# A hybrid diffusion backbone: transposes of the modulation chunks in a rotating PSUM bank

## The chip, the cores and the metric

The kernel runs on one core of one Trainium2 chip. The metric is the device time of one execution in microseconds (us); the number of a kernel is the median of its runs. The engines are called by the names of the profile: PE (matmul), PEld (its weight load), DVE, ACT, POOL, and the queues that issue DMAs (SPq, ACTq).

## The reference

One inference step through two layers of a diffusion backbone with a model width of 2048. There are 256 tokens: 128 of context and 128 latent ones. Cut to what matters here:

```
for l in range(2):
    mods = SiLU([c_ctx, c]) @ ada_w[l] + ada_b[l]      # 2 x 12288: shift, scale, gate, twice
    u    = rmsnorm(x) * (1 + scale1) + shift1
    p    = u @ w_in[l]                                 # columns of three head groups
    y    = [attention(p), gated_delta_rule(p), ssd_scan(p)]
    x    = x + gate1 * (concat(y) @ w_out[l])
    x    = x + gate2 * swiglu_ffn(rmsnorm(x) * (1 + scale2) + shift2)
```

The modulation is a product of two rows (one for context tokens, one for latent tokens) with a 2048 x 12288 matrix per layer, 96 MB of weights in each layer. The other weights (`w_in`, `w_out`, the feed-forward matrices) are streamed from HBM too, and each is used once.

## The kernel before, in words

**Weights.** A weight tile (`raw`, 512 KB) is loaded through SPq into a ring of four. ACT copies it into a rounded tile (L360), DVE or POOL takes the residual (L364), and PE multiplies the tokens with both into one of four PSUM banks `acc`. These matmuls, `acc<-h,w` in the profile, fill most of PE's time.

**Modulation.** Its columns are cut into 48 chunks of 256 columns for each layer. The first 16 of layer 0 are done ahead of the layer, most of the others as sums on DVE. The 24 chunks 16 to 39 of layer 0 are done on PE in the mixers of layer 0, between other work. One chunk is 16 matmuls `ada<-araw,sc`: four weight tiles `araw` of 512 KB with four matmuls each (`ada_run`). The four row groups of the result land in the first half of one PSUM bank, `pz["sums"]`, whose tile is named `ada`. Then ACT copies the sums to one buffer `adsb` in SBUF (L422), and the chunk is pending. `ada_flush` finishes a pending chunk: two PE transposes of `adsb` (L435) into a PSUM tile `pm`, a DVE reduction into `mods` (L436), a DVE sum with the bias (L437).

**When chunks run.** `tick` is called in the loops of the mixers: it flushes the pending chunk and then runs more of the next one by a credit. The matmul stream of the program, DVE's and the other engines' are then ordered by a scheduler, which places each instruction from what it needs and what is free; so a changed dependency can change the order of an engine. What this order is can be listed without running the kernel.

**The `araw` tiles.** There are eight of them: two in the pool of the weights and six in a pool `am`, which is released at the end of the delta rule. The tiles of the attention part (`cr`, `sqa`, `sqb`) then take its place, so the DVE copies of attention's first projection (L1178) wait until the last of the six has been read. From there on two tiles are left.

**PSUM.** Eight banks: four of `acc`, one of the sums, three that rotate, allocated by `mx()`. All the small products of the mixers (state-space scan, delta rule, attention) use the three, each tile until its reader has finished.

**The mixers in order of time (layer 0).** The state-space scan (`u,xd` and `bt,xd` products, from 204 us); inputs of the delta rule: norms by `t,ones`, ACT L613, decay factors `E` (DMA L874, DVE L879), then `Bp` (DVE L1039); its 16 x 16 inverse, done by DVE alone (L1047 to L1058), with transfers to DRAM and back on both sides (`sB`, `Lr` ahead, `sZ`, `sW`, `Z`, `W` behind); the solve, a chain of `Z,Bp`, `t,W` and `W,t` products (L1094 to L1111) with chunks between; outputs (`E,Z`, `qe,s`, `t,ones`); then attention (`sqa,ones`, `usT,cst`, `krd,cst`).

Of the kernel before, what the change touches and what calls it, by code (L numbers as in the profile page):

```python
# [182 lines left out]
def build(tc, nc, a):  # L183
# [5 lines left out]
    def nm(s):  # L189
        uid[0] += 1  # L190
        return f"{s}_{uid[0]}"
# [6 lines left out]
    pz = {}  # L198
# [16 lines left out]
    def mx():  # L215
        return pz["mx"].tile([128, 512], F32, name=nm("mx"), tag="mx")
# [60 lines left out]
    def C(name):  # L277

        if name == "ident":
            return ident  # L280
        o, w = _COFF[name]
        return cst["t"][:, o:o + w]
# [5 lines left out]
    def cr(l, name, n):  # L288
        o = _COLS[name]
        return cols[:, l, o:o + n]  # L290
# [107 lines left out]
    def ada_run(n):  # L398


        i = ada_state["i"]
        if i >= ada_state["stop"]:
            return
        l, c = ada_q[i]
        if ada_state["u"] == 0:
            ada_state["ps"] = pz["sums"][:, 0:256]
        ps = ada_state["ps"]
        ada_fetch(n - len(ada_state["raws"]))

        for u in range(ada_state["u"], ada_state["u"] + n):  # L410
            raw = ada_state["raws"].pop(0)
            for j in range(4):
                mm(ps[32 * j:32 * j + 32], sc[:, 4 * u + j, :], raw[:, j, :], u == 0, u == 3)
                pinned["on"] = True
        pinned["on"] = False
        ada_state["u"] += n
        if ada_state["u"] == 4:
            ada_flush()
            ada_state["u"] = 0
            ada_state["i"] += 1  # L420
            sb = wp.tile([128, 256], F32, name=nm("adsb"), tag="adsb", bufs=1)
            S.activation(sb, ps, AF.Copy)  # L422
            ada_state["pend"] = l, c, sb

    def ada_flush():

        if ada_state["pend"] is None:
            return
        l, c, sb = ada_state["pend"]
        ada_state["pend"] = None  # L430
        pm = pz["sums"][:, 256:512]
        md = mods[l][:, 2 * c:2 * c + 2, :]
        bias = cr(l, "adab", 96)[:, 2 * c:2 * c + 2].unsqueeze(2).to_broadcast([128, 2, 2])
        for t in range(2):
            PE.transpose(pm[:, t * 128:(t + 1) * 128], sb[:, t * 128:(t + 1) * 128], C("ident"))  # L435
        V.tensor_reduce(md, pm.rearrange("p (t j r) -> p t r j", t=2, j=4)[:, :, 0:2, :], axis=AX.X, op=ALU.add)  # L436
        V.tensor_tensor(md, md, bias, op=ALU.add)  # L437
        scale_rows(l, 2 * c, 2 * c + 2)

    def scale_rows(l, a0, a1):  # L440

        for w, o in enumerate((16, 64)):
            b0, b1 = max(a0, o), min(a1, o + 16)
            if b0 < b1:
                gain = cr(l, "n1" if w == 0 else "n2", 16)[:, b0 - o:b1 - o].unsqueeze(2).to_broadcast([128, b1 - b0, 2])
                V.scalar_tensor_tensor(modA[l][w][:, b0 - o:b1 - o, :], mods[l][:, b0:b1, :], 1.0, gain, op0=ALU.add, op1=ALU.mult)
# [84 lines left out]
    def tick(n=1.0):  # L531
        credit[0] += rate[0] * n
        if "s" in pz:
            while credit[0] >= 1.0:
                credit[0] -= 1.0
                vec_step()
            return
        ada_flush()
        while credit[0] >= ada_state["run"]:
            credit[0] -= ada_state["run"]  # L540
            ada_run(ada_state["run"])
# [33 lines left out]
    def ada_until(l, c):  # L575

        while ada_state["i"] < ada_state["stop"] and ada_q[ada_state["i"]] < (l, c):
            ada_run(2)
        if ada_state["pend"] is not None and ada_state["pend"][:2] < (l, c):
            ada_flush()  # L580
# [1007 lines left out]
```

## Time and profile before

| | |
|---|---|
| median of three runs | 2791.19 us (2787.31 to 2797.09) |
| profiled execution | 2789.01 us, span 2787.2 us, 1.8 us around the span |
| PE busy | 2624.7 us, 94% of the span |
| DVE, ACT, POOL busy | 1924.1, 1261.9, 753.6 us |
| matmuls of the chunks, `ada<-araw,sc` | 88.3 us on PE, with 21.1 us of idle time before them |
| mixers of layer 0, where the chunks run | 204 to about 670 us of the span |

How to read it: PE's share is so high that the time is PE's work and PE's waits. The idle time before the chunk matmuls is the time in which PE had arrived at such a matmul and could not start it. The profile counts each 32-bit matmul in two records, so that one chunk is 32 records of `ada<-araw,sc`.

### The profile page before, as it was taken

The numbers are of one execution on the slowest core, as the hardware profiler recorded it, in microseconds if no ns is written. First come the engines' busy times: TensorE is split into PE (matmuls) and PEld (weight loads), VectorE is DVE, ScalarE is ACT, GpSimd is POOL, SyncE is SP. The second block draws the span as 40 slices with busy tenths as digits, with TensorE's granted clock in tenths as the row PEclk, the third lists the DMA queues.
The fourth block names the chain that finished last, engine by engine and source line by source line (L and its number), as shares of the span: only waits on it lengthen the run. The fifth ranks groups of instructions, "written<-read, shape, count | busy, mean of one in ns | idle before, by whom it ended". The sixth has DMA issues, their size and how long they took to land. (4 is left out here: it accounts for less than half of the span.)

```text
span 2787.2 us, 45955 instructions
## 1 busy us (share of the span) xinstructions
PE 2624.7 (94%) x17856; PEld 2324.3 (83%) x17856; DVE 1924.1 (69%) x3162; ACT 1261.9 (45%) x1802; POOL 753.6 (27%) x415
## 2 busy tenths in 40 slices
PE   7988889999999999999999999999999999999999
PEld 5876767888887788788888888888988888888888
DVE  2657845454999899898986786555477777755444
ACT  4345605544444444444334563355454454444333
POOL 1121003222455555455554320231330000000000
PEclk9999999999999999999999999999999999999999
DMA  8988757456698888889985555343657777655554
GB/s 331 347 305 289 251 185 243 151 212 222 230 323 313 312 299 318 294 307 337 340 322 186 172 163 169 111 137 110 221 194 230 232 241 229 202 187 188 195 195 149
DMA packets 224107, 658.01 MB, mean 236 GB/s; under 512 B 34320, under 2 KB 61584, under 8 KB 223888
## 3 DMA queue, kind: packets, MB, share of 16 engines
q1 hardware_dynamic: 174384, 619.26, 64.1%
q10 hardware_dynamic: 49504, 35.81, 4.3%
q8 instruction: 140, 2.29, 0.3%
q14 instruction: 79, 0.65, 0.1%
HBM read 641.22 MB, written 13.76 MB: 235 GB/s over the span
## 5 line engine op out<-in xcount | busy, mean ns | idle before, releaser
L225 PE MATMUL acc<-h,w 128*128 128x256 f32 (+1 forms) x8960 | 1428.9, 320 | 54.2 <-DVE w L364 19.0
L225 PEld LDWEIGHTS acc<-h,w 128*128 128x128 f32 x8960 | 1273.2, 193 | 205.6 <-DVE w L364 29.0
L360 ACT ACTIVATE w<-raw 128x1024 fp32r<-128x1024 f32 (+2 forms) x811 | 828.6, 1025 | 889.1 <-PE acc L225 606.5
L364 DVE TENSOR_TENSOR w<-raw,w 128x1024 fp32r<-128x1024 f32 (+2 forms) x577 | 710.5, 1232 | 512.5 <-ACT w L360 503.6
L364 POOL TENSOR_TENSOR w<-raw,w 128x1024 fp32r<-128x1024 f32 (+3 forms) x234 | 569.2, 2434 | 993.1 <-ACT w L360 840.2
L505 DVE SCALAR_TENSOR_TENSOR junk<-araw,srep 128x1024 bf16<-128x1024 f32 x448 | 544.5, 1215 | 9.6 <-DMA araw<-ada_w 1.9
L225 PE MATMUL acc<-f,w 128*128 128x256 f32 (+1 forms) x2560 | 456.3, 340 | 3.6 <-DVE w L364 3.6
L225 PEld LDWEIGHTS acc<-f,w 128*128 128x128 f32 x2560 | 392.8, 189 | 64.3 <-DVE w L364 4.3
L225 PE MATMUL acc<-m,w 128*128 128x256 f32 x1536 | 191.8, 285 | 0.0
L225 PEld LDWEIGHTS acc<-m,w 128*128 128x128 f32 x1536 | 186.6, 192 | 2.9 <-issue 2.5
L1424 POOL TENSOR_TENSOR f<-sg,f 128x512 fp32r<-128x512 f32 x40 | 60.9, 1523 | 426.3 <-ACT f L1423 426.3
L225 PE MATMUL ada<-araw,sc 128*32 128x256 f32 x1280 | 88.3, 397 | 21.1 <-DVE mods L436 16.2
L225 PE MATMUL mx<-h,w 128*128 128x256 f32 (+1 forms) x672 | 90.7, 293 | 10.1 <-ACT w L360 5.2
L225 PEld LDWEIGHTS mx<-h,w 128*128 128x128 f32 (+1 forms) x672 | 85.7, 195 | 14.6 <-ACT w L360 6.2
L661 DVE SCALAR_TENSOR_TENSOR xT<-acc,mods,xT 128x128 f32<-128x128 f32 x192 | 53.9, 343 | 43.1 <-PE acc L225 35.5
L225 PEld LDWEIGHTS ada<-araw,sc 128*32 128x32 f32 x1280 | 37.6, 112 | 51.8 <-DVE mods L436 18.1
L1428 ACT ACTIVATE up<-acc 128x256 f32<-128x256 f32 x80 | 30.7, 384 | 107.6 <-PE acc L225 76.4
L648 ACT ACTIVATE h<-nt,mods 128x128 fp32r<-128x128 f32 x128 | 44.0, 392 | 63.7 <-DVE nt L647 62.5
L647 DVE SCALAR_TENSOR_TENSOR nt<-xT,modA,rstd 128x128 f32<-128x128 f32 x128 | 57.0, 482 | 7.4 <-ACT rstd L611 7.2
L1428 ACT ACTIVATE sg<-acc 128x256 f32<-128x256 f32 x80 | 29.9, 381 | 68.4 <-PE acc L225 68.4
L602 POOL TENSOR_TENSOR sqacc<-sqacc,sqt 128x256 f32<-128x256 f32 x39 | 39.9, 1022 | 74.0 <-ACT sqt L598 73.1
L1463 DVE TENSOR_TENSOR sg<-sg,up 128x256 f32<-128x256 f32 x80 | 57.8, 723 | 1.6
(296 smaller groups left out, 1971.6 us busy)
## 6 DMA issues: line engine op xcount, KB each, us to landing
araw<-ada_w SPq DMA_DIRECT2D x384, 512.0 KB, 5.4
raw<-ffn_w_gu SPq DMA_DIRECT2D x352, 512.0 KB, 4.4
raw<-ffn_w_down SPq DMA_DIRECT2D x165, 512.0 KB, 4.3
raw<-w_in SPq DMA_DIRECT2D x144, 512.0 KB, 4.6
raw<-w_out SPq DMA_DIRECT2D x64, 512.0 KB, 4.0
raw<-mla_w_uq SPq DMA_DIRECT2D x24, 384.0 KB, 3.1
raw<-mla_w_ukv SPq DMA_DIRECT2D x16, 512.0 KB, 3.7
araw<-srow SPq DMA_DIRECT2D x12, 512.0 KB, 5.7
```

Source lines behind the costliest of these rows:

```text
L225: return pin(PE.matmul(out, lhsT=lhsT, rhs=rhs, start=start, stop=stop, skip_group_check=True))
L360: S.activation(w1[:, :w], raw[:, :w], AF.Copy)
L364: e.tensor_tensor(w2[:, :w], raw[:, :w], f32(w1[:, :w]), op=ALU.subtract)
L505: V.scalar_tensor_tensor(junk, raw, 1.0, s[r], op0=ALU.mult, op1=ALU.mult, accum_out=sums[g][:, 2 * (c - g[1]) + t, r, h:h + 1]))
L602: G.tensor_tensor(sq["acc"], sq["acc"], t, op=ALU.add)
L647: V.scalar_tensor_tensor(t[:, c], X_["t"][:, kt, c], A[:, kt, g:g + 1], rstd[:, c], op0=ALU.mult, op1=ALU.mult)
L648: S.activation(h1[:, kt, c], t[:, c], AF.Identity, bias=B[:, kt, g:g + 1])
L661: V.scalar_tensor_tensor(xs, ps[:, i * T:(i + 1) * T], gates[:, kt, g:g + 1], xs, op0=ALU.mult, op1=ALU.add)
L1424: G.tensor_tensor(f[:, :, 1], sg_, f32(f[:, :, 0]), op=ALU.subtract)
L1428: S.activation(t, bank[:, NT:2 * NT], AF.Copy)
L1463: V.tensor_tensor(t[:, j], t[:, j], u, op=ALU.mult)
```

## The change

The PSUM tile that takes the two transposes of a finished chunk is no longer the second half of the bank of the running sums; it is a fresh tile of the three rotating banks. Nothing else in the text of the program differs:

```
 def ada_flush():
     ...
     l, c, sb = ada_state["pend"]
     ada_state["pend"] = None
-    pm = pz["sums"][:, 256:512]
+    pm = mx()[:, 0:256]
     md = mods[l][:, 2 * c:2 * c + 2, :]
     ...
     for t in range(2):
         PE.transpose(pm[:, t * 128:(t + 1) * 128], sb[:, t * 128:(t + 1) * 128], C("ident"))
     V.tensor_reduce(md, pm.rearrange(...), axis=AX.X, op=ALU.add)
```

The counts of instructions are the same, but for two table loads fewer on ACT. The order of the engines changes in the mixers of layer 0; from their end on it is the same. Three places follow; a suffix such as `x4` is the number of matmuls, and numbers behind names count tiles.

The first is PE around the wait for the inverse: the last inputs `qT,kT`, and the first product of the solve, `Z,Bp`. Before:

```order
L435 MATMUL ada_70<-ident,adsb_3216 128x128 x2
L225 MATMUL ada_70<-araw_3274,sc 32x256 x4
L225 MATMUL ada_70<-araw_3276,sc 32x256 x4
L225 MATMUL ada_70<-araw_3278,sc 32x256 x4
L225 MATMUL ada_70<-araw_3280,sc 32x256 x4
L435 MATMUL ada_70<-ident,adsb_3298 128x128 x2
L225 MATMUL ada_70<-araw_3455,sc 32x256 x4
L225 MATMUL ada_70<-araw_3457,sc 32x256 x4
L225 MATMUL ada_70<-araw_3459,sc 32x256 x4
L225 MATMUL ada_70<-araw_3461,sc 32x256 x4
L225 MATMUL mx_3006<-Z_2936,Bp_2839 128x128 x4
L225 MATMUL mx_3013<-t_3011,W_2937 128x128 x4
```

And now:

```order
L225 MATMUL mx_2999<-qT_244,kT_245 128x128 x4
L225 MATMUL mx_3006<-qT_244,kT_245 128x128 x4
L225 MATMUL acc_4087<-h_236,w_667_4332 128x256 x2
L225 MATMUL acc_4087<-h_236,w_668_4333 128x256
L225 MATMUL mx_3013<-Z_2943,Bp_2846 128x128 x4
L225 MATMUL mx_3020<-t_3018,W_2944 128x128 x4
L225 MATMUL mx_3026<-W_2944,t_3018 128x128 x4
L435 MATMUL mx_3032<-ident,adsb_2708 128x128 x2
L225 MATMUL mx_3037<-Z_2947,Bp_2859 128x128 x4
L225 MATMUL ada_70<-araw_3201,sc 32x256 x4
L225 MATMUL ada_70<-araw_3203,sc 32x256
```

Three chunks with two pairs of transposes stood between `qT,kT` and the solve (the first chunk is just above the rows); now none stands there, and the transposes in the solve come a product or two later than the copy they need.

The second place is PE at the end of the delta rule, from the last products `E,Z` over the second pair of `t,ones`. Before:

```order
L225 MATMUL mx_3365<-E_2878,Z_2948 128x128
L225 MATMUL ada_70<-araw_3964,sc 32x256 x3
L225 MATMUL ada_70<-araw_4132,sc 32x256 x4
L225 MATMUL acc_4349<-h_236,w_655_4352 128x256
L225 MATMUL acc_4349<-h_236,w_656_4353 128x256
L225 MATMUL mx_3384<-t_3382,ones 128x512
L225 MATMUL acc_4349<-h_236,w_655_4352 128x256 x2
L225 MATMUL acc_4349<-h_236,w_656_4353 128x256
L225 MATMUL acc_4349<-h_236,w_658_4370 128x256 x2
L225 MATMUL acc_4349<-h_236,w_659_4371 128x256
```

And now:

```order
L225 MATMUL mx_3394<-t_3392,ones 128x512
L435 MATMUL mx_3431<-ident,adsb_3308 128x128 x2
L435 MATMUL mx_3522<-ident,adsb_3490 128x128 x2
L225 MATMUL ada_70<-araw_3557,sc 32x256 x4
L225 MATMUL ada_70<-araw_3559,sc 32x256 x4
L225 MATMUL ada_70<-araw_3561,sc 32x256 x4
L225 MATMUL ada_70<-araw_3563,sc 32x256 x4
L435 MATMUL mx_3613<-ident,adsb_3581 128x128 x2
L225 MATMUL ada_70<-araw_3618,sc 32x256 x4
L225 MATMUL ada_70<-araw_3620,sc 32x256 x4
L225 MATMUL ada_70<-araw_3622,sc 32x256 x4
L225 MATMUL ada_70<-araw_3624,sc 32x256 x4
```

What was done a few matmuls at a time between the outputs now stands in one piece: the piece goes on for two and a half more chunks, 72 chunk matmuls and six pairs of transposes in all, before the next `acc` matmul.

The third place is ACT around the second of the two L613, which make the norms of `qT`; the DMAs L874 fetch the rows from which the decay factors `E` are made. Before:

```order
L360 ACTIVATE w_650_4315<-raw_4313 128x1024
L613 ACTIVATE t_2813<-t_2813,lnq 128x512
L609 ACTIVATE t_2820<-mx_2822,eps 128x512
L881 ACTIVATE E_2832<-E_2832 128x512
L613 ACTIVATE t_2820<-t_2820,lnq 128x512
L881 ACTIVATE E_2845<-E_2845 128x512
L1035 ACTIVATE qe_2865<-E_2863 128x512
L874 DMA E_2878<-gcd 128x512
```

And now:

```order
L609 ACTIVATE t_2827<-mx_2829,eps 128x512
L613 ACTIVATE t_2820<-t_2820,lnq 128x512
L613 ACTIVATE t_2827<-t_2827,lnq 128x512
L874 DMA E_2839<-gcd 128x512
L360 ACTIVATE w_659_4260<-raw_4258 128x1024
L874 DMA E_2852<-gcd 128x512
L874 DMA E_2870<-gcd 128x512
L874 DMA E_2885<-gcd 128x512
L360 ACTIVATE w_662_4290<-raw_4288 128x1024
L881 ACTIVATE E_2839<-E_2839 128x512
```

All four fetches of `E` now stand behind the second L613; three of them stood well ahead of it.

## Rows read from the trace of the kernel before

**Rows 1.** The page, part 5: the chunk matmuls on PE

```profile
L225 PE MATMUL ada<-araw,sc 128*32 128x256 f32 x1280 | 88.3, 397 | 21.1 <-DVE mods L436 16.2
```

**Rows 2.** PE's waits, 200 to 470 us: total, times, longest

```profile
PE ada L225 <- DVE mods L436: 16.2, 8, 4.7
PE mx L225 <- DMA Z<-sZ: 6.4, 1, 6.4
PE ada L225 <- DMA araw<-ada_w: 4.0, 4, 1.9
```

**Rows 3.** PE's timeline in the scan: start, duration, records, idle before

```profile
214.46 3.64 PE L225 MATMUL ada<-araw,sc 128*32 128x256 f32 x32 [2.74 <-DVE mods L436]
```

**Rows 4.** Windows: PE, PEld, DVE, ACT, POOL busy (records), clock, DMA share, GB/s

```profile
214.00:224.00 10.00, 9.24 (x57) 6.75 (x58) 6.65 (x23) 5.97 (x11) 2.37 (x1) 0.51 0.73 267
224.00:234.00 10.00, 10.00 (x101) 8.94 (x100) 8.07 (x17) 5.86 (x10) 1.40 (x1) 1.00 0.83 274
...
314.00:324.00 10.00, 10.00 (x77) 9.04 (x76) 5.37 (x4) 9.94 (x13) 2.37 (x1) 1.00 0.45 147
...
428.00:442.00 14.00, 11.31 (x102) 9.49 (x99) 5.72 (x10) 4.91 (x7) 2.97 (x3) 1.00 0.98 337
```

**Rows 5.** ACT's groups by line, 204 to 324 us

```profile
L360 ACT ACTIVATE w<-raw 128x1024 fp32r<-128x1024 f32 x23 | 24.1, 1050 | 12.2 <-PE acc L225 12.2
L605 ACT ACT_TABLE_LOAD x6 | 7.7, 1283 | 0.1
```

**Rows 6.** ACT's timeline at the second L613

```profile
322.87 0.71 ACT L613 ACTIVATE t<-t,lnq 128x512 f32<-128x512 f32 x1
```

**Rows 7.** DVE's timeline: last Bp, and end of the inverse

```profile
333.98 1.12 DVE L1039 SCALAR_TENSOR_TENSOR Bp<-mx,beta,E 128x128 f32<-128x128 f32 x4
...
350.85 0.38 DVE L1058 COPY Ln<-X 128x256 f32<-128x256 f32 x1
```

**Rows 8.** Tile E, 285 to 340 us: its fetches

```profile
DMA to landing us min/median/max: 3.7/5.6/6.2
```

**Rows 9.** PE's timeline from the wait for the inverse into the solve

```profile
342.08 3.64 PE L225 MATMUL ada<-araw,sc 128*32 128x256 f32 x32 [4.67 <-DVE mods L436]
346.28 0.63 PE L435 MATMUL ada<-ident,adsb 128*128 128x128 f32 x2 [0.55 <-ACT adsb L422]
347.83 1.93 PE L225 MATMUL ada<-araw,sc 128*32 128x256 f32 x32 [0.92 <-DVE mods L436]
...
351.36 1.93 PE L225 MATMUL ada<-araw,sc 128*32 128x256 f32 x32 [0.65 <-DVE mods L436]
359.66 2.08 PE L225 MATMUL mx<-Z,Bp 128*128 128x128 f32 x8 [6.37 <-DMA Z<-sZ]
363.42 2.05 PE L225 MATMUL mx<-t,W 128*128 128x128 f32 x8 [1.68 <-DMA W<-sW]
...
368.93 1.16 PE L225 MATMUL mx<-t,W 128*128 128x128 f32 x8 [0.57 <-DVE t L1101]
...
380.66 0.44 PE L435 MATMUL ada<-ident,adsb 128*128 128x128 f32 x2 [0.49 <-ACT adsb L422]
```

**Rows 10.** DMA issues, 334 to 364 us: count, size, median us to landing

```profile
Z<-sZ ACTq DMA_DIRECT2D x4, 256.0 KB, 6.9
...
sB<-Bp ACTq DMA_DIRECT2D x1, 256.0 KB, 2.3
...
Lr<-sB ACTq DMA_DIRECT2D x1, 128.0 KB, 3.0
sZ<-X ACTq DMA_DIRECT2D x1, 64.0 KB, 5.8
```

**Rows 11.** Tile araw, 362 to 410 us: its 13 loads

```profile
DMA to landing us min/median/max: 3.4/3.6/7.7
```

**Rows 12.** PE's timeline in attention

```profile
447.21 7.82 PE L225 MATMUL acc<-h,w 128*128 128x256 f32 x63
458.33 0.46 PE L225 MATMUL mx<-krd,cst 128*128 128x128 f32 x2 [3.29 <-DVE krd L1230]
```

More of the change, by code (lines that the diff above doesn't have):

```diff
@@ L430, in ada_flush @@
         ada_state["pend"] = None
-        pm = pz["sums"][:, 256:512]
+        pm = mx()[:, 0:256]
         md = mods[l][:, 2 * c:2 * c + 2, :]
```

## The prediction

> **What bounds the kernel now.** I start from the page: PE is busy 94% of the span, so what a change to PE's waits is worth must be read where PE waits. The costliest groups show the one wait that the change speaks of: before the chunk matmuls PE sat idle for 21.1 us in all, 16.2 us of it until DVE had reduced the chunk before (L436) [rows 1]. The list of PE's waits in the mixers of layer 0 shows that these are eight waits and that none lies elsewhere [rows 2]. The reason is the shared bank: the next chunk's matmuls write the bank from which DVE still has to read the transposes, and DVE has a long queue. 16.2 us are 0.58% of the time. This is the most that the edit can take away directly.
>
> PE's timeline tells where the eight are. Three lie in the wait for the inverse: 4.67, 0.92 and 0.65 us [rows 9]. There PE has nothing else to do, since behind them stands a wait of 6.37 us for the transfer of `Z` [rows 9]; taking these 6.2 us away gains nothing. The other five, 16.2 − 6.2 = 10.0 us, lie in the state-space scan and the delta rule's inputs, the first of them 2.74 us long [rows 3]. After this first one the granted clock is 0.51 for a slice of 10 us, the lower of the two levels, and back at full in the next [rows 4]: 57 records there against 101 in the next slice. At the next slice's rate 57 records take 5.6 us, so 4.4 us more go with this wait.
>
> Then I ask what ends the stretch. Up to the last `Bp` (ends at 333.98 + 1.12 = 335.1 us [rows 7]) PE's arrears delay everything, but near its end ACT is busy 9.94 of 10 us [rows 4], and the last part is a chain from the second L613 (322.87 [rows 6]) to the last `Bp`, 12.2 us. From 335.1 on it is a chain again: inverse, transfers, solve, outputs.
>
> **The change part by part.** All sums are against the profiled execution, 2789.0 us, which is 2.2 us under the median of before. The order of the engines is the larger part of this change, so each term follows it. I write Δ for how much earlier the last `Bp` ends.
>
> *Waits in the scan.* 10.0 us of waits and 4.4 us of lower clock go, if the transposes in a rotating bank let PE run on: −14.4. Bounds: nothing, if the wait only moves to another instruction, and 14.4.
>
> *ACT up to the second L613.* By the new order it has three weight copies fewer ahead of it (18 instead of 21, 1.05 us each [rows 5]) and two table loads fewer (1.28 each [rows 5]): 5.7 us less. It is the full engine only in the last part of the stretch, so I take half, −2.9, between 0 and −5.7.
>
> *The fetches of `E`.* All four now stand behind the second L613, and a fetch takes 3.7 us at the least, 5.6 in the middle [rows 8]. Before, half of the decay factors were ready by then. The 3.7 us are new; eight more DVE instructions at 0.28 us (four `Bp` take 1.12 [rows 7], and I take `E` for the same) are 2.2 us, and about 1 us of other work fits into the landing: +4.8, between +3.7 and +7.
>
> So Δ = 14.4 + 2.9 − 4.8 = 12.5 us, with bounds from below zero to 16.4.
>
> *The wait for the inverse.* Three chunks (16 matmuls take 1.93 us at full clock [rows 9]) and two pairs of transposes (0.27 each, an estimate from the 0.44 of one pair [rows 9] less its pipelined end) have left it: 3 × 1.93 + 0.5 = 6.3 us of PE's work that was free there must now be done elsewhere, +6.3. On the other side their eight-tile ring was being refilled in that wait, and the transfers of the inverse ran beside it: from the end of the inverse at 350.85 [rows 7] to the first `Z,Bp` at 359.66 [rows 9] are 8.8 us, for two hops with medians of 5.8 and 6.9 us to landing, while the two hops ahead of the inverse, with SPq quiet, took 2.3 and 3.0 [rows 10]. With 0.2 us for the second issue that is 5.5 us: −3.3, between 0 and −3.3. The 1.68 us for `W` [rows 9] come from the same crowd; I take half, −0.8.
>
> *The solve.* Four times the transposes there held up the chain, once by 0.57 and three times by 0.49 us, of which one row stands for three [rows 9]. Now they stand after their copy: −2.0.
>
> *The piece behind the last `t,ones`.* 72 chunk matmuls (8.7 us at 1.93 for 16) and six pairs of transposes (1.6 us) now stand there without other work between. Eight tiles are loaded ahead, two chunks; the other ten must come after the first is read. A load took 3.6 us alone [rows 11], and when loads queue, the core got 337 GB/s [rows 4], 1.56 us for 512 KB. The piece begins with two hops through the single `adsb`, 1.3 us by the 0.49 and 0.55 us of such waits [rows 9] and their transposes; the first tile is free 0.5 us later; then 3.6 + 9 × 1.56 + 0.5 us to the end of the last matmul: 19.9 us for 10.3 us of work, so +9.6. Bounds: +2.8, if the tiles kept up and only five copies at 0.55 us stood in the way, and +13.7 with the slowest landing of [rows 11].
>
> *Attention.* Before, chunks there waited 4.0 us for tiles, 3.0 of them after the outputs (four waits in all [rows 2]). As many chunk matmuls follow the piece as stood there before, but on tiles ordered earlier: half returns, −1.5, between 0 and −3. Lastly `krd,cst` now stands behind 42 `acc` matmuls where it stood behind 63, and it already waited 3.29 us [rows 12]: 21 × 0.124 (7.82 / 63 [rows 12]) = 2.6 us of cover are gone, +2.6.
>
> The sum: −12.5 + 6.3 − 3.3 − 0.8 − 2.0 + 9.6 − 1.5 + 2.6 = −1.6 us, which is 2787.4 against the profiled execution and 2789.6 against the median. I forecast 2789.
>
> A rule of the Trainium skill speaks against the first term: TensorE: Matmul & The Clock Gate, A second HAM failure mode: psum-queue depth-cycling, tells of a kernel in which going through the PSUM banks with small idle times made the clock swing between its levels. By it the 4.4 us of lower clock would stay, and the sum would be +2.8. The first row of [rows 4] agrees that a short wait can bring the lower level; no row shows it for the use of more banks.
>
> **The rivals.**
>
> *Faster: the tiles keep up.* If the ring is served as fast as PE asks, the piece costs only its copies (+2.8 instead of +9.6), and if ACT's whole 5.7 us count, Δ is 2.8 us larger. Then −1.6 − 6.8 − 2.8 = −11.2, about 2780. For it: DMA is little used in the stretches where the ring would fill, 0.45 in [rows 4]. Against it: the ring holds two chunks and the piece asks for four and a half.
>
> *Slower: the wait moves to the next user of a rotating bank.* DVE is as late as before, and its reduction now holds one of three banks that every product of the scan needs. With two banks left, PE would stop at the next `u,xd` in place of the next chunk. If all 14.4 us stay, the sum is +12.8, about 2804; it decides (slower by over 8.4 us, 0.3%) from 10.0 of the 14.4. For it: the eight waits are DVE's lag, which the edit doesn't shorten. Against it: the flush is now placed several matmuls later in the scan, between the `u,xd` groups.
>
> The Trainium skill has a measurement on this side: in TensorE: Matmul & The Clock Gate, its section on the thin case of few rows, adding PSUM double-buffering gave no further gain. By it the 10.0 us of waits would come back elsewhere; no run here shows it yet.
>
> *The piece cools the clock.* PE works half of the time in it. After the waits at 342.08 sixteen matmuls took 3.64 instead of 1.93 us [rows 9]; if the `acc` work behind the piece starts so, a slice like that of 0.51 [rows 4] costs another 4.4 us, and with the slowest loads (+4.1) the sum is +6.9, about 2798, within 0.3%.
>
> *The edit doesn't do what it says.* The chunk before still has to leave the sums by ACT's copy into a single `adsb`, which waits for the transposes before it. If every freed wait became one of 0.55 us for this copy, five of them are 2.8 us: +1.2, about 2792.
>
> **How the numbers follow.** My forecast with its own range (2781 to 2797, all within 0.3%, about what a measurement of this kernel can tell from no change) has 0.45; the cool clock 0.10 and the copy 0.10 lie within it too. Faster has 0.19, slower 0.16. So same is 0.65. The range must leave out at most 2 in 10: it reaches to the far side of most of the faster case, 2778, and into the slower one, 2803.
>
> **What would show it.** In the changed profile no wait of PE should end on L436 in the scan, and the slice around 214 to 224 us should have the full clock. The last `Bp` should end near 323 us. PE should be idle for about 19 us ahead of the first `Z,Bp`, and the two hops should land in 2 to 3 us each. The solve should have no wait on `adsb`. Behind the second `t,ones` there should be a piece of about 20 us with waits for `araw` that sum to some 7 us and copies for the rest. I am wrong if Δ is under 3 us, if the piece takes under 14 us, or if a wait on DVE appears in the products of the scan.

## The result, and the profile after

The changed kernel takes 2807.48 us (median of 8 runs, 2803.4 to 2814.62) against 2790.47 us before (8 runs): a ratio of 1.0059 with a 95% interval of [1.0039, 1.0079]. It is slower, by some 17 us. The forecast was 2789 us and no change; its range ended at 2803. The profiled execution is the longest of the eight, 2814.62 us with a span of 2812.8. It is 25.6 us over the profiled execution of before, where the medians are 17 us apart, so the sizes read from the two profiles below are those of this pair.

The list of PE's waits in the changed kernel, for the same mixers as in [rows 2] (columns: total, times, longest):

```profile
PE mx L225 <- DMA Z<-sZ: 19.9, 1, 19.9
PE mx L225 <- DVE u L961: 8.0, 3, 3.9
PE ada L225 <- DMA araw<-ada_w: 7.6, 8, 1.9
PE mx L225 <- issue: 5.6, 1, 5.6
PE mx L225 <- DVE krd L1230: 3.8, 1, 3.8
PE mx L435 <- ACT adsb L422: 3.3, 5, 0.8
```

No wait ends on L436 any more: the edit does what it says. But two rows have grown, `issue` to 5.6 us and `u L961` to 8.0, and the wait for `Z` is 19.9 us long where it was 6.4. The two rows before:

```profile
PE mx L225 <- DVE u L961: 1.1, 1, 1.1
PE mx L225 <- issue: 0.3, 1, 0.3
```

PE's timeline shows where the longer waits of the scan are (start, duration, records, idle before):

```profile
217.84 1.06 PE L225 MATMUL mx<-da,cst 128*128 128x48 f32 x4 [5.64 <-issue]
...
242.41 0.66 PE L225 MATMUL mx<-u,xd 128*64 128x128 f32 x8 [3.88 <-DVE u L961]
...
273.99 0.70 PE L225 MATMUL mx<-u,xd 128*64 128x128 f32 x4 [3.38 <-DVE u L961]
```

And DVE's timeline shows what they wait for, and where the last `Bp` ends:

```profile
217.53 0.21 DVE L842 TENSOR_TENSOR da<-sp,nega 128x48 f32<-128x48 f32 x1
...
335.21 0.86 DVE L1039 SCALAR_TENSOR_TENSOR Bp<-mx,beta,E 128x128 f32<-128x128 f32 x3
...
352.08 0.37 DVE L1058 COPY Ln<-X 128x256 f32<-128x256 f32 x1
```

The product `da,cst` starts 0.1 us after DVE has made `da`; the list puts its wait down to `issue`, but this row shows that it is one for DVE. Before the change the product started at 218.91, and PE had waited 2.74 us for L436 at the chunk just ahead of it; now PE comes to the product earlier and waits there. The last `Bp` ends at 335.21 + 0.86 = 336.1 us; before, it was 335.1 [rows 7].

PE's timeline from the wait for the inverse on, to compare with [rows 9]:

```profile
358.58 2.05 PE L225 MATMUL mx<-Z,Bp 128*128 128x128 f32 x8 [19.90 <-DMA Z<-sZ]
361.41 2.08 PE L225 MATMUL mx<-t,W 128*128 128x128 f32 x8 [0.78 <-DVE t L1101]
...
419.46 1.12 PE L225 MATMUL mx<-t,ones 128*128 128x512 f32 x2 [0.69 <-ACT t L1145]
420.42 0.38 PE L435 MATMUL mx<-ident,adsb 128*128 128x128 f32 x2
421.63 0.44 PE L435 MATMUL mx<-ident,adsb 128*128 128x128 f32 x2 [0.83 <-ACT adsb L422]
422.00 1.93 PE L225 MATMUL ada<-araw,sc 128*32 128x256 f32 x32
...
430.49 0.64 PE L225 MATMUL ada<-araw,sc 128*32 128x256 f32 x8 [0.82 <-DMA araw<-ada_w]
...
435.98 0.64 PE L225 MATMUL ada<-araw,sc 128*32 128x256 f32 x8 [1.78 <-DMA araw<-ada_w]
438.52 2.31 PE L225 MATMUL ada<-araw,sc 128*32 128x256 f32 x16 [1.91 <-DMA araw<-ada_w]
...
442.01 1.93 PE L225 MATMUL ada<-araw,sc 128*32 128x256 f32 x16
443.88 5.00 PE L225 MATMUL acc<-h,w 128*128 128x256 f32 x25
...
467.50 0.70 PE L225 MATMUL mx<-usT,cst 64*128 64x256 f32 x2
477.18 0.46 PE L225 MATMUL mx<-krd,cst 128*128 128x128 f32 x2 [3.76 <-DVE krd L1230]
```

The wait for the inverse is empty, and the piece behind the second `t,ones` takes 443.88 − 420.42 = 23.5 us. The stretches between the same marks, before and after, in us:

| stretch | before | after |
|---|---|---|
| up to the last `Bp` (from the span's start) | 335.1 | 336.1 |
| to the first `Z,Bp` | 24.6 | 22.5 |
| solve, to `vt,W` | 47.2 | 45.8 |
| outputs, to the second `t,ones` | 17.3 | 15.1 |
| piece and attention, to `usT,cst` | 22.4 | 48.0 |
| to `krd,cst` (63 `acc` matmuls before, 42 after) | 11.7 | 9.7 |

The sum is 477.18 − 458.33 = 18.9 us, and the 21 `acc` matmuls that are still to come are another 2.6. The other 4 us between the two profiled executions lie behind these marks.

### The profile page after: what moved, and what is told of

It is laid out like the page before. It is cut to its first block, busy times and chain, and to the rows that moved or that the text cites. A ratio compares the mean times of both kernels' runs of the same rounds, so it can differ in the third digit from the quotient of the medians.

```text
span 2812.8 us, 45932 instructions
## 1 busy us (share of the span) xinstructions
PE 2631.0 (94%) x17856; PEld 2329.0 (83%) x17856; DVE 1919.2 (68%) x3162; ACT 1259.6 (45%) x1800; POOL 756.3 (27%) x415
## 5 line engine op out<-in xcount | busy, mean ns | idle before, releaser
L225 PE MATMUL acc<-c,w 128*128 128x256 f32 x288 | 55.2, 287 | 2.8 <-ACT r L1258 2.8
```

What stands on the lines that cost most here:

```text
L225: return pin(PE.matmul(out, lhsT=lhsT, rhs=rhs, start=start, stop=stop, skip_group_check=True))
```

## The experiments

Two theories stood after the result. **The turn of the banks:** a tile of the rotating banks is handed out in the order of the program, in turn with all small products of the mixers. A chunk that needs one can't run ahead of the products that stand before it, so the scheduler can no longer put it into the wait for the inverse, and everything that was held back comes in one piece behind the last `t,ones`. The waits of the scan are worth nothing, since PE only comes earlier to products that wait for DVE. **The scan's banks** (the slower rival of the prediction, taken further): the loss is made in the scan, where DVE's late reduction holds one of three banks.

**Half of the change, twice.** The bank is chosen by the stage; the second kernel has the opposite condition.

```
-        pm = pz["sums"][:, 256:512]
+        pm = mx()[:, 0:256] if ada_state.get("g") is None else pz["sums"][:, 256:512]
 ...
+            ada_state["g"] = 1          # end of the scan
             ada_pace(TM[1][0], TM[1][1], 4)
```

In the scan only:

> The transposes use a rotating bank in the state-space scan only, and the bank of the sums from the end of the scan on. Theory 1 (the turn of the banks): a tile of the rotating banks is handed out in turn with the small products of the program, so a chunk cannot run ahead of products that stand before it; the loss comes from the delta rule, where this empties the wait for the inverse and makes the piece behind the last t,ones. Then this kernel has three chunks in that wait and no piece, and its time is that of before within 0.3% (2783 to 2796 us), with the waits of the scan moved to the products that need DVE's own results (da, u L961). Theory 2 (the scan's banks): the loss is in the scan, where DVE's late reduction holds one of three banks; then this kernel keeps most of the loss, 2800 us or more, and is slower by over 0.3%.

In the delta rule and attention only:

> The other half alone: the bank of the sums in the scan, a rotating bank from the end of the scan on. Theory 1: the whole loss stays, 2803 to 2815 us: no chunk in the wait for the inverse, and a piece of 20 to 24 us behind the second t,ones. The eight waits on L436 in the scan are five again. Theory 2: little of the loss stays, 2786 to 2797 us.

Measured: in the scan only 2791.43 us, ratio 1.001 [0.9989, 1.0032]; from the scan's end on 2815.58 us, 1.0099 [1.0071, 1.0127]. The first keeps three waits on L436, those in the wait for the inverse, and has the longer ones of the scan nearly in full. Its list of waits:

```profile
PE mx L225 <- DVE u L961: 6.8, 3, 3.5
PE ada L225 <- DVE mods L436: 6.2, 3, 4.3
PE mx L225 <- issue: 5.6, 1, 5.6
```

The second has the emptied wait and the piece, here in its timeline on PE:

```profile
359.00 2.04 PE L225 MATMUL mx<-Z,Bp 128*128 128x128 f32 x8 [20.29 <-DMA Z<-sZ]
...
439.28 2.30 PE L225 MATMUL ada<-araw,sc 128*32 128x256 f32 x16 [1.47 <-DMA araw<-ada_w]
```

The whole loss lies behind the scan. The second kernel is even 8 us slower than the full change, just over the range expected; why isn't shown. (Its waits on L436 in the scan are three, not the five expected: 6.9 us.)

**A bank outside the turn, and its price.** The eight banks are full, so one is taken from the rotating three.

```
-        pz["mx"] = tc.alloc_tile_pool(name=nm("ps_mx"), bufs=3, space=PSUM, reuse_waits="tile")
+        pz["mx"] = tc.alloc_tile_pool(name=nm("ps_mx"), bufs=2, space=PSUM, reuse_waits="tile")
+        pz["tp"] = tc.alloc_tile_pool(name=nm("ps_tp"), bufs=1, space=PSUM, reuse_waits="tile")
 ...
-        pm = pz["sums"][:, 256:512]
+        pm = pz["tp"].tile([128, 512], F32, name=nm("tp"), tag="tp")[:, 0:256]
```

> The transposes get a bank of their own, outside the turn of the others, and the small products keep two rotating banks in place of three. Theory 1: chunks can again run ahead, no wait ends on L436, the wait for the inverse is full of chunks and there is no piece; if two banks cost nothing, 2778 to 2790 us, otherwise that plus their price (next run). Theory 2 has two banks for the products of the scan here too, so that they wait for DVE more than in the changed kernel: 2805 us or more.

The second kernel has the first line alone (`bufs=2`):

> The kernel before, with two rotating banks in place of three; nothing else. It is the price that the run with a bank of its own pays. Theory 1: within 0.3% of before to 10 us over it, since the new order is that of before but for a few chunk matmuls. Theory 2: 2800 us or more, since the scan's products wait for a bank.

Measured: 2802.01 us, 1.0039 [1.0017, 1.006] with a bank of its own; 2805.59 us, 1.0069 [1.0042, 1.0096] for two banks alone. Two banks cost some 14 us, more than I had expected by the turn of the banks, and inside the range that the scan's banks had given. But the profile doesn't put the price in the scan: from the first transposes of `usT` (L815, the scan's start) to the last `Bp` it takes 131.6 us, before 131.0. Part of the price lies ahead of the scan (PE's waits for `kT L747`, all of them there, are 8.9 us, six of them, where before they were 1.5 us, one), part behind it (the first `Z,Bp` starts 29.3 us after the last `Bp`, before 24.6). The two intervals overlap, so the times alone don't settle what a bank of its own is worth. The profile of the kernel with a bank of its own does settle the order of the instructions: no wait ends on L436, the wait for the inverse is full of chunks again and there is no piece. A row from PE's timeline ahead of its first `Z,Bp`, and the row of that product:

```profile
350.88 1.07 PE L227 MATMUL ada<-araw,sc 128*32 128x256 f32 x16
...
364.20 2.08 PE L227 MATMUL mx<-Z,Bp 128*128 128x128 f32 x8 [5.13 <-DMA Z<-sZ]
```

**No transposes at all.** DVE reduces the SBUF copy; the modulation of these chunks is made of wrong columns.

```
-        pm = pz["sums"][:, 256:512]
+        pm = sb[:]
 ...
-        for t in range(2):
-            PE.transpose(pm[:, t * 128:(t + 1) * 128], sb[:, t * 128:(t + 1) * 128], C("ident"))
```

> The kernel before without the two transposes of each chunk: DVE reduces the copy in SBUF instead, so no PSUM tile is needed for a finished chunk (the modulation of these chunks is then made of the wrong columns). It bounds what any other place for the transposes could bring. If the scan is paced by DVE and not by PE's waits on L436, the last Bp still ends at 331 to 337 us and the time is 2780 to 2792 us. If PE's waits pace the scan, as the prediction had it, the last Bp ends near 323 us and the time is 2770 to 2780 us.

Measured: 2797.69 us, 1.002 [1.0003, 1.0037]; the last `Bp` ends at 336.33 + 1.12 = 337.5 us. Even with no PSUM tile for the transposes the last `Bp` doesn't come earlier. The time is above what I had expected and says little on the scan, since it carries a loss of its own: the first `Z,Bp` starts 34.1 us behind the last `Bp`, before 24.6. PE now waits on ACT's copies, most of it once in the wait for the inverse:

```profile
PE ada L225 <- ACT adsb L422: 13.5, 6, 10.9
```

**The piece without its loads.** For chunks 28 to 32 the changed kernel reads weight tiles that are already in SBUF, so that 20 loads and these values are left out.

```
+            if l == 0 and 28 <= c < 33:
+                ada_state["raws"].append(ada_state["last"][u % 2])
+                ada_state["f"] += 1
+                continue
             with tc.high_priority():
                 raw = ada_tile()
```

> The changed kernel, in which five chunks of the piece behind the last t,ones read weight tiles that are already there in place of their own (their 20 loads are left out, and their values are wrong). The order around the wait for the inverse is unchanged; the piece is one chunk longer. If the piece is long because its loads come one behind the other, it takes about 16 us with no wait on araw, and the time falls by 6 to 11 us to 2796 to 2802 us. If something else holds up what follows the piece, the time stays at 2803 us or more.

Measured: 2800.15 us, 1.0032 [1.0018, 1.0045], 7 us under the changed kernel. PE's timeline of the piece, now 88 chunk matmuls:

```profile
417.99 0.38 PE L440 MATMUL mx<-ident,adsb 128*128 128x128 f32 x2
...
428.43 1.93 PE L225 MATMUL ada<-araw,sc 128*32 128x256 f32 x32
430.93 0.44 PE L440 MATMUL mx<-ident,adsb 128*128 128x128 f32 x2 [0.56 <-ACT adsb L427]
...
435.16 10.32 PE L225 MATMUL acc<-h,w 128*128 128x256 f32 x84
```

It takes 435.16 − 417.99 = 17.2 us where 16 were expected, each chunk with one wait of 0.56 to 0.84 us for the copy. The granted clock (the column ahead of the DMA share) stays at 1.00, the higher of its two levels, in the piece and behind it:

```profile
417.00:430.00 13.00, 10.19 (x140) 5.13 (x140) 3.04 (x13) 2.64 (x6) 0.00 (x0) 1.00 0.14 38
430.00:442.00 12.00, 10.87 (x117) 8.60 (x110) 5.42 (x12) 5.76 (x11) 5.12 (x4) 1.00 0.62 175
```

In the changed kernel it is full in the first half of the piece, with waits for tiles of up to 0.85 us, and falls in the second half, where they reach 1.78 and 1.91 us (first half, second half, and the stretch behind the piece):

```profile
421.00:432.00 11.00, 6.90 (x97) 2.97 (x97) 2.54 (x11) 1.87 (x5) 0.00 (x0) 1.00 0.74 258
432.00:444.00 12.00, 7.04 (x61) 2.07 (x61) 3.42 (x8) 1.85 (x4) 1.27 (x1) 0.73 0.68 258
444.00:455.00 11.00, 10.39 (x77) 8.64 (x78) 4.13 (x7) 4.30 (x8) 3.88 (x3) 0.82 0.81 253
```

**Fewer chunks up to the end of the delta rule, with either bank.** The same line in the changed kernel and in the kernel before:

```
-TM, TF = ((24, 8), (32, 12.8), (40, 76)), (255, 140)
+TM, TF = ((24, 8), (27, 12.8), (40, 76)), (255, 140)
```

In the changed kernel:

> The changed kernel with five chunks fewer for the delta rule and five more for attention (27 in place of 32 in the table of the pace). By its order there is no piece any more, and the wait for the inverse is still empty. If the loss is the piece and the emptied wait, about 13 us come back and about 5 stay: 2792 to 2800 us. If attention, with its two tiles, can't hide five more chunks, 2803 us or more.

In the kernel before:

> The kernel before (transposes in the bank of the sums) with 27 in place of 32 chunks up to the end of the delta rule: the control of the run with fewer chunks, which differs from this one in the bank alone. By its order chunks and acc matmuls fill the wait for the inverse and the solve, and no piece follows. If the change costs what it empties, this kernel is faster than that run by 6 us or more, at 2785 to 2797 us; and faster than before by up to 5 us if the two tiles of attention keep up. If moving five chunks is what costs there, this kernel is as slow as that run, 2800 us or more.

Measured: 2803.96 us, 1.0039 [1.0025, 1.0053] with the rotating bank; 2776.82 us, 0.9952 [0.9935, 0.997] with the bank of the sums. The first falls short of what I had expected and lies where attention could not hide five more chunks. The second has the same five there and is better than expected: with five chunks fewer the sums' bank wins some 14 us, and this version beats both kernels (what brings this gain wasn't tried). So moving five chunks is not by itself what costs. With the rotating bank the wait for the inverse stays empty (19.8 us for `Z`), and PE's work in the 80 us around wait and solve shows the difference, 55.75 us against 68.70 (first the rotating bank, then the bank of the sums; columns as in [rows 4]):

```profile
340.00:420.00 80.00, 55.75 (x442) 49.27 (x443) 39.77 (x83) 7.17 (x13) 2.56 (x2) 0.85 0.21 57
```

```profile
340.00:420.00 80.00, 68.70 (x578) 54.89 (x578) 45.54 (x97) 9.88 (x18) 3.82 (x3) 0.91 0.54 163
```

**What paces the scan.** The first attempt moved weight residuals from DVE to POOL:

```
-        turn[1] = P_Q
+        turn[1] = P_Q if l else 0.8
```

> The kernel before, with four of five weight residuals of the scan and the delta rule's inputs in layer 0 on POOL, in place of one of two; PE's order is that of before. If DVE's queue paces the scan, DVE sheds some 6 to 9 us, the last Bp ends 3 to 9 us earlier and the time is 2781 to 2788 us. If ACT or PE paces it, or the slower residuals on POOL come too late, 2789 us or more.

It tells nothing on its question, as the setting is overwritten before it takes effect: the order of all engines is that of before. As a second measurement of the same program it is useful: 2795.52 us, 1.0011 [0.9995, 1.0026], and its last `Bp` ends at 332.0 us, 3.1 us from that of before. So much two executions differ at this mark. The setting that does take effect (`turn[1] = P_G if l else 0.8`), in the kernel before:

> The kernel before, with four of five weight residuals of the stretch up to the inverse on POOL in place of one of three (the setting that takes effect there; three fewer stand on DVE before the inverse, and more acc work is placed in the scan). If DVE's queue paces the scan, the products da and u,xd start earlier by the residuals that left their front, and the time is 2780 to 2788 us. If the scan is a chain through DVE, ACT and transfers, in which no queue alone is full, the time is that of before within 0.3%.

And with the transposes in a rotating bank in the scan only:

> The same setting with the transposes in a rotating bank in the scan only. If PE's waits on L436 come back in value once DVE is less full, this one is faster than the run before it by 3 to 10 us; if they are worth nothing at all, the two are equal within 0.3%.

Measured: 2800.53 us, 1.0042 [1.0023, 1.0061], and 2800.8 us, 1.0034 [1.0018, 1.0051]. Both are slower, which neither reading had expected, and the last `Bp` ends past 342 us. POOL needs 2434 ns for a residual where DVE needs 1232 (the page of before); that this is the reason isn't shown. The two are equal: without the waits on L436 nothing is gained here either.

**The turn, with another ring.** To see it at work, the transposes go into the four `acc` banks:

```
-        pm = pz["sums"][:, 256:512]
+        pm = acc()[:, 0:256]
```

> The kernel before, with the transposes in one of the four acc banks, which are handed out in turn with the weight matmuls. By the theory of the turn the weight matmuls can then not run ahead of the chunks: by its order no acc matmul is left in the scan, so PE is idle there for some 50 us, and the time is 2830 us or more. If sharing a ring with later work did no harm, it is 2790 to 2805 us.

Measured in one run: 2831.3 us. No `acc` matmul runs in the scan now, and PE works only 23.67 of 40 us there. A window, two of its waits, and the last `Bp` on DVE:

```profile
240.00:280.00 40.00, 23.67 (x247) 13.99 (x247) 23.88 (x67) 16.18 (x28) 0.44 (x2) 0.79 0.74 256
```

```profile
PE mx L225 <- DVE u L961: 15.7, 4, 6.8
PE mx L225 <- issue: 7.8, 1, 7.8
```

```profile
310.21 3.96 DVE L1039 SCALAR_TENSOR_TENSOR Bp<-mx,beta,E 128x128 f32<-128x128 f32 x15
```

It ends at 310.21 + 3.96 = 314.2 us, 21 us earlier than before (18 us, counted from the scan's start). So the scan is not a fixed chain: the `acc` work beside it, with its copies and residuals on ACT and DVE, holds it up by that much. Which of these engines does isn't shown.

## Why the prediction was wrong

**The step that failed is the first term: "10.0 us of waits and 4.4 us of lower clock go, if the transposes in a rotating bank let PE run on: −14.4."** The waits went, and the last `Bp` ends at 336.1 instead of the 322.6 that Δ = 12.5 asked for. PE's idle time came back at the products for which DVE has to make an operand, 5.64 us at `da,cst` (before 0.30) and 8.0 at `u,xd` (before 1.1). This is the prediction's own sign of being wrong, a wait on DVE in the products of the scan. I had named this in the slower rival as the next user of a rotating bank; it is rather the next user of DVE's work, since what PE waits for is `da` and `u`, not a bank. The last `Bp` shows it over eight traces. With waits on L436 in the scan it ends at 335.1, 332.0, 333.8 and 336.5 us (before, the same program again, the delta rule half, fewer chunks in the kernel before); without them at 336.1, 329.6, 333.8 and 334.6 (changed, scan half, no loads, fewer chunks). The means are 334.4 and 333.5. The scan's start (the first transposes of `usT`) itself differs by 6.9 us between these traces (198.1 to 205.0), as much as such a gain. Counted from it, the last `Bp` ends after 131.0, 133.8, 130.8 and 131.5 us with the waits, and after 133.1, 131.5, 132.8 and 132.6 without them: nothing has come through to this mark. And `da,cst` starts 14.8 us behind the scan's start in all eight, whether PE waited for L436 ahead of it or not. What I read wrongly is in [rows 2]: a wait of PE was taken for time of the program, without asking what the next product behind it waits for. The lower clock didn't go either, it moved: 0.66 in 214 to 224 us, where it was 0.51, and 0.84 in 274 to 284, which had 1.00 (two rows of the changed kernel, then one of before):

```profile
214.00:224.00 10.00, 6.16 (x34) 6.16 (x35) 7.04 (x19) 5.18 (x10) 2.38 (x1) 0.66 0.62 229
274.00:284.00 10.00, 10.00 (x102) 8.52 (x102) 8.28 (x21) 8.21 (x13) 0.00 (x0) 0.84 0.91 325
```

```profile
274.00:284.00 10.00, 8.98 (x101) 6.48 (x101) 5.66 (x12) 7.15 (x11) 0.00 (x0) 1.00 0.96 379
```

The 4.4 us were also read too high: in their slice PE is busy 9.24 of 10 us [rows 4], so 0.8 us of them are idle time, and part of that is already in the 10.0.

**The part of ACT and of `E`.** The second L613 ended earlier, at 316.91 + 0.72 instead of 322.87 + 0.71:

```profile
316.91 0.72 ACT L613 ACTIVATE t<-t,lnq 128x512 f32<-128x512 f32 x1
```

These are 6.0 us (1.1 of them lie ahead of the scan), close to the 5.7 us of ACT's work that the order takes away, but without the 14.4 on top: of the 17.3 us that the two terms put at this mark at most 6 came. In the eight traces the second L613 ends 114.1 to 114.9 us behind the scan's start without the waits and 119.5 to 123.0 with them, but the four without them have the new order of ACT too (18 or 19 weight copies ahead of it for 21). The kernel with a bank of its own has no wait on L436 and 24 copies there, and takes 120.5. That speaks for ACT's work and against the waits, though no run changes the one without the other. From there to the last `Bp` it is 336.1 − 316.9 = 19.2 us instead of 12.2: +7.0, the upper bound of the price for the fetches of `E` and not the 4.8 taken (whose parts, 3.7 + 2.2 − 1, make 4.9). So what was gained at L613 was lost again in the fetches of `E` behind it. With a bank of its own, where the fetches stand well ahead of the second L613, the last `Bp` ends 5.3 us after it, 125.9 us behind the scan's start (131.6 with two banks alone).

**The wait for the inverse and the solve** were right in kind. The chunks left the wait, the transfers are quicker (2.6 us for `sZ`, 6.5 in place of 8.8 us in all, so −2.3 for the −3.3 expected), and no transposes hold up the solve; but six waits of 0.78 and 0.22 us for DVE's `t`, 3.0 us in all, took part of that place, and the solve is 1.4 us shorter, not 2.8. The 0.57 us that I counted among the transposes' waits was such a wait for `t` already [rows 9].

**The piece** was priced too low: 23.5 us for 19.9. Waits for tiles are 5.8 us and those for copies 3.3. The lower clock doubled the time of the last two groups of the piece (2.31 and 1.93 us, where 16 records take 1.07 at full clock) and made the 25 `acc` matmuls behind it take 5.0 us for 3.1. I had this as a rival of its own (the piece cools the clock), and the run without loads shows that it comes with the waits for tiles: without them the clock stays full. **`krd,cst`** waited 0.5 us longer, for 2.6 expected.

So by the marks: −12.5 became +1.0, and the stretch of the piece and attention, which the terms put at +18.4 (8.7 + 1.6 + 9.6 − 1.5), became +25.6. These two are 20.7 of the 23.1 us between −1.6 and +21.5 (18.9 up to `krd,cst` and the 2.6 still to come).

**What the loss is.** The halves show that all of it comes from the delta rule on, and the runs with 27 chunks show what the bank costs where no piece follows: 1.0039 against 0.9952, some 24 us between two kernels that differ in the bank alone. So a piece isn't needed for a loss of this size; what the bank empties ahead of it is enough there. The mechanism (tiles of a ring come in the order of the program) is seen in the order of the instructions and in the ring of `acc`. How the 17 us of the change itself divide between the emptied wait and the piece isn't settled: the loads of the piece are some 7 us of them, and the rest wasn't tried apart.

The Trainium skill advises, in Perfetto Trace Analysis, Matmuls, to let independent matmul groups rotate through different PSUM banks, so that the evacuation of one overlaps the next. Here the measurement is on the other side, 1.0059: the groups were independent only as long as they did not share the ring.

## What to carry to other kernels

A buffer of its own lets work be moved; a ring that is shared with other work fixes its place in the program's order. Before a tile is given to a ring, ask which of its users have to run ahead of which. And a wait that a profile lists is worth removing only if the next thing behind it doesn't wait for the same engine: look up when the operands of the next dependent product are made.

## What was not expected of the hardware

Two executions of one and the same program differ by 5.9 us at the start of the scan (204.10 and 198.24) and by 3 us at its end (335.1 and 332.0), while `da,cst` starts 14.8 us after the first transposes of `usT` in both; a single mark, counted from the start of one profile, should not carry a gain of this size. And with 20 loads less the same piece of small matmuls ran at a granted clock of 1.00, where waits for tiles of up to 1.91 us between its matmuls had gone with 0.73.
